# Stick-breaking attention: the scans' second operand moves to a PSUM column, and ScalarE copies the sums

## The chip, the cores and the metric

The kernel runs on one core of one Trainium2 chip. The metric is device time in microseconds (us), the median of the runs. The engines' names are those of the profile: PE (TensorE's matmuls), PEld (its weight loads), DVE (VectorE), ACT (ScalarE), POOL (GpSimd), SP (SyncE, which issues every DMA). PE writes only to PSUM, an accumulator memory of eight banks of 2 KB in each partition; DVE and ACT read it.

## The reference

One encoder layer for 2048 new frames (with 16 meta tokens ahead of them) and 64 frames of a running stream with 2048 cached ones: a combined projection, then two groups of heads, then an output projection and a gated ConvFFN. What matters here is group A, the stick-breaking attention: eight heads of 64, strictly causal, without a softmax.

```
z = (q @ k^T) * 64 ** -0.5                      # mask: key s < query t
log_1m = where(mask, log_sigmoid(-z), 0)
later  = cumsum(log_1m, reverse) - log_1m       # sum over the keys between s and t
a = where(mask, exp(log_sigmoid(z) + later), 0)
out = a @ v
```

So a weight is sigmoid(z) times the product of sigmoid(-z) over all keys that lie between key and query. Group B, the retention (four heads of 128), is a chunked recurrence and needs the same normalised input.

## The kernel before

The frames are stored newest first, so that the running product goes forward along a row. A matrix product at full precision is three matmuls of a high and a low part.

The stages follow each other: projections of q, k and v (to about 350 us), then a stage in which attention and retention are woven into one instruction stream (about 350 to 1320 us), then the rest of the retention with the output projection, then the ConvFFN. Every engine's queue is in program order, and the program order is written by hand: `attention()` and `retention()` are generators that yield the nanoseconds of PE work that they have just emitted, and `interleave` takes a step of retention (650 to 1300 ns nominal) whenever attention has got ahead of a fixed share, 0.82.

Attention is a list of 237 units: `Meta`, 20 `Samp` units (the running stream) and 216 `Prompt` units, one for a pair of heads p, a block I of 256 queries, a head e of the pair and a chunk of 512, 256 or 272 keys. By shape these are 48 units of 512 keys, 48 of 256 and 56 of 272 that continue a row, and 24 of 512, 32 of 256 and 8 of 272 that begin it (diagonal chunks, in which the second tile of queries skips 128 keys). A prompt unit goes through these steps:

- `z` (L1080 and after): for each of two tiles of 128 queries the matmuls of q and k into a PSUM tile `z` (L1094, L1095, L1097), then two sigmoids on ACT (`sigmoids`, L888), which write `sn` (of -z) and `sp` (of z) to SBUF. There is a yield behind each tile. Then comes `products`: two running products on DVE (`tensor_tensor_scan`, L898), one for each tile, and two multiplications `sp * pr` on POOL (L904).
- `t`: PE transposes the weights (L1123, L1126) into PSUM tiles `tt`; ACT copies each to `ahi` (L1116) and DVE makes the rest `alo` (L1117).
- `av`: 4 to 8 matmuls (L1157) add weights times values into `o`, a PSUM tile of 128x256 from the one-buffer pool `p_o`. Behind the last chunk of a row DVE copies `o` to `os` in SBUF (L1162), and the next row's first matmul has to wait for this copy.

The steps of different units are interleaved at fixed distances:

```
z = units[s].z() if 0 <= s < N else iter(())
yield next(z, 0)
for lag, what in ((3, "t"), (0, "z"), (4, "av"), (4, "fin"), (-2, "pre")):
```

So in program order the scans of unit s stand directly ahead of the `av` matmuls of unit s-4, and between `z` of the second tile and these scans stands at most what `interleave` puts at one yield. The scan computes state = data0 * state and bypasses its second operand, `data1`; before the change `data1` is `sn`, the same SBUF row as `data0`. The framework derives the semaphore waits from the tiles that instructions read and write.

Of the kernel before, what the change touches and what calls it, by code (L numbers as in the profile page):

```python
# [8 lines left out]
F32 = mybir.dt.float32  # L9
F32R = mybir.dt.float32r  # L10
BF16 = mybir.dt.bfloat16
AF = mybir.ActivationFunctionType
# [35 lines left out]
def hybrid_layer(ctx: ExitStack, tc: tile.TileContext, a):  # L48
# [5 lines left out]
    V, S, G, PE = nc.vector, nc.scalar, nc.gpsimd, nc.tensor  # L54
# [12 lines left out]
    def pool(stack, name, bufs, side="left", space=None):  # L67
        kw = {"space": space} if space is not None else {}
        return stack.enter_context(tc.tile_pool(name=name, bufs=bufs, reuse_waits="tile", side=side, **kw))
# [67 lines left out]
    while t > 0:  # L137
        n = min(GB, t)
# [533 lines left out]
    with ExitStack() as st:  # L672
# [10 lines left out]
        p_z = pool(st, "p2z", 2, space=PSUM)  # L683
        p_t = pool(st, "p2t", 2, space=PSUM)
        p_o = pool(st, "p2op", 1, space=PSUM)
        cos_t, sin_t, s_ret, tri_t = (p2[n] for n in ("cos", "sin", "s", "tri"))
        snr = [cp.tile([128, 2, 520], F32, name=f"sn{n}") for n in range(2)]
        qzs = [cp.tile([128, 2, 256], F32R, name=f"qz{n}") for n in range(3)]
# [123 lines left out]
        def attention():  # L812
# [4 lines left out]
            def piece_of(c):  # L817
                return min(c // 512, NPC - 1)
# [19 lines left out]
            def load_v(p, j):  # L838
                c0, c1 = edges[j], edges[j + 1]
                t0 = c0 // 128  # L840
                n = (c1 - c0) // 128
                vt = kvp.tile([128, -(-(c1 - c0) // 128), 256], F32R, name="vt", tag=f"v{j}")
                dma(out=vt[:, :n], in_=d_v[p, :, t0:t0 + n])
                if (c1 - c0) % 128:

                    G.memset(f32(vt[:, n]), 0.0)
                    dma(out=vt[:META, n], in_=d_v[p, :META, t0 + n])
                vpt[p, j] = vt

            def free_pieces(I):  # L850
                nxt = 256 * (I + 1)
                return [j for j in range(NPC) if edges[j + 1] == nxt or (nxt == SEQ and edges[j + 1] == KT)]
# [17 lines left out]
            class Breaks:  # L870
# [19 lines left out]
                def products(self, carry, nj=1):  # L890
                    n, sn, sp = self.n, self.sn, self.sp
                    pr = ppp.tile([128, 2, 520], F32, name="pr", tag="pr")
                    for j in range(nj):
                        s = self.skip * j
                        if s:
                            V.memset(pr[:, j, s:s + 1], 1.0)
                            s += 1
                        V.tensor_tensor_scan(  # L898
                            out=pr[:, j, s:n + 1], data0=sn[:, j, s:n + 1], data1=sn[:, j, s:n + 1],
                            initial=1.0 if carry is None else carry[:, j, 0:1], op0=ALU.mult, op1=ALU.bypass,  # L900
                        )
                    for j in range(nj):
                        c = slice(self.skip * j, n)
                        G.tensor_tensor(out=sp[:, j, c], in0=sp[:, j, c], in1=pr[:, j, c], op=ALU.mult)  # L904
                    return sp, pr[:, :, n:n + 1]
# [8 lines left out]
            class Meta:  # L914
# [21 lines left out]
                    yield 110  # L936

                def av(self):
                    self.o = p_o.tile([128, 256], F32, name="o", tag="o")
                    for p in range(NP):  # L940
                        PE.matmul(
                            self.o[32 * p:32 * p + 32, 0:128], lhsT=self.at[:, 32 * p:32 * p + 32],
                            rhs=v_last[0:META, 128 * p:128 * p + 128], start=True, stop=True,
                            tile_position=(0, 32 * p),
                        )
                    self.os = op.tile([128, 256], F32, name="os", tag="os", bufs=3)
                    V.tensor_copy(self.os[:, :128], self.o[:, :128])
                    yield 400
# [22 lines left out]
            def load_cv(g, j):  # L971
                cv = kvp.tile([128, 2, 4, 128], F32, name="cv", tag=f"v{j}")
                for e in range(2):
                    dma(out=cv[:, e], in_=a["cv"][2 * g + e, :, 4 * j:4 * j + 4])
                cvs[g, j] = cv

            class Samp:
# [45 lines left out]
                def av(self):  # L1023
                    p, c, st = self.p, self.c, self.st
                    if c == 0:
                        st["o", p] = p_o.tile([128, 256], F32, name="o", tag="o")
                        o = st["o", p]
                        PE.matmul(
                            o[:, :128], lhsT=self.at[:DEC, 0], rhs=v_samp[:, 128 * p:128 * p + 128],
                            start=True, stop=False,  # L1030
                        )
                    else:
                        o = st["o", p]
                        for b in range(4):
                            PE.matmul(
                                o[:, :128], lhsT=self.at[:, b], rhs=cvs[p // 2, c - 1][:, p % 2, b],
                                start=False, stop=c == NC and b == 3,
                            )
                        if p == 1:
                            load_cv(1, c - 1)  # L1040
                        elif p == 3 and c <= NPC:
                            load_v(0, c - 1)
                    if c == NC:
                        self.os = op.tile([128, 256], F32, name="os", tag="os", bufs=3)
                        V.tensor_copy(self.os[:, :128], o[:, :128])
                    yield 900
# [11 lines left out]
            class Prompt:  # L1058
# [80 lines left out]
                def av(self):  # L1139
                    p, e, st = self.p, self.e, self.st  # L1140
                    if self.c == 0:
                        st["o", e] = p_o.tile([128, 256], F32, name="o", tag="o")
                    o = st["o", e]
                    j0 = piece_of(self.start)
                    vt = vpt[p, j0]
                    b0 = (self.start - edges[j0]) // 128
                    seq = list(range(self.nb)) + ([self.nb] if self.rem else [])
                    if self.c == 0:
                        seq = seq[1:] + [0]
                    for x, b in enumerate(seq):  # L1150
                        w = 128 if self.c == 0 and b == 0 else 256
                        first = self.c == 0 and x == 0
                        end = self.c == self.nch - 1 and x == len(seq) - 1
                        vs = vt[:, b0 + b, 128 * e:128 * e + 128]
                        for z, src in enumerate((self.hi, self.lo)):
                            rhs = src[:, b].rearrange("p j c -> p (j c)")[:, :w]
                            PE.matmul(o[:, :w], lhsT=vs, rhs=rhs, start=first and z == 0, stop=end and z == 1)  # L1157
                        if x % 2 == 1:
                            yield 440
                    if self.c == self.nch - 1:  # L1160
                        self.os = op.tile([128, 256], F32, name="os", tag="os", bufs=3)
                        V.tensor_copy(self.os, o)  # L1162
                        if e == 1 and p + 1 < NP:
                            for j in free_pieces(self.I):
                                load_v(p + 1, j)
                    yield 220 * (len(seq) % 2)
# [21 lines left out]
            st = {}  # L1188
# [3 lines left out]
            for p in range(NP):  # L1192

                for I in [0] + list(range(NQ - 1, 0, -1)) if p == NP - 1 else range(NQ):
                    st = {}
# [600 lines left out]
```

## Time and profile before

| what | before |
|---|---|
| median of 3 runs (lowest, highest) | 3060.58 us (3058.88, 3062.67) |
| profiled execution, its span | 3063.43 us, 3061.7 us |
| PE busy | 2952.8 us, 96% |
| PEld busy | 2626.5 us, 86% |
| DVE busy | 2043.5 us, 67% |
| POOL busy | 1602.7 us, 52% |
| ACT busy | 1506.9 us, 49% |
| granted TensorE clock, mean | 0.991 |

Busy is the time in which an engine executed something. Matmuls are pipelined, so a matmul's record is longer than the distance to the next one; a busy PE is not PE at its peak. The granted clock is a share of 2.4 GHz. A timeline row gives the start in us from the span's start, the duration of what it merges, the engine, the line, the operation, what it wrote and read, and in brackets the idle time of the engine before it and what ended it.

### The profile page before, as it was taken

How to read it: one execution, taken by the hardware profiler on the slowest of the kernel's cores; microseconds unless marked ns; L12 is line 12 of the kernel's file. 1: busy time of each engine (PE TensorE's matmuls, PEld its weight loads, DVE VectorE, ACT ScalarE, POOL GpSimd, SP SyncE). 2: the span in 40 equal slices, each digit the busy share in tenths (PEclk: the TensorE clock that was granted, in tenths of full speed). 3: DMA queues.
4: the chain of work that ended last, by engine and by line, in shares of the span. 5: the costliest groups of instructions: out<-in, count | busy, mean ns of one | idle time of the engine just before them, and what ended most of it. 6: DMA issues, size and time to landing. Idle time of an engine off the chain costs nothing. (4 is left out here: it accounts for less than half of the span.)

```text
span 3061.7 us, 48809 instructions
## 1 busy us (share of the span) xinstructions
PE 2952.8 (96%) x16834; PEld 2626.5 (86%) x16834; DVE 2043.5 (67%) x3027; ACT 1506.9 (49%) x3331; POOL 1602.7 (52%) x1817
## 2 busy tenths in 40 slices
PE   7999999899999999999999999999999999999998
PEld 6888688788878878878789998789999889999887
DVE  3331368888888888854346666768888667888622
ACT  5332456666666666643334444454444444444433
POOL 1220377778778777753324445434446343455543
PEclk9999999999999999999999999999999999999999
DMA  6765753433343443247645556645555655455644
GB/s 224 279 221 178 263 176 104 134 119 105 122 136 103 126 129 107 75 173 252 212 155 178 185 176 229 199 158 152 154 157 170 220 187 164 148 146 155 212 156 149
DMA packets 278355, 512.07 MB, mean 167 GB/s; under 512 B 36612, under 2 KB 118404, under 8 KB 266204
## 3 DMA queue, kind: packets, MB, share of 16 engines
q1 hardware_dynamic: 278108, 508.95, 51.5%
q8 instruction: 134, 2.20, 0.3%
q14 instruction: 113, 0.93, 0.1%
HBM read 371.63 MB, written 137.09 MB: 166 GB/s over the span
## 5 line engine op out<-in xcount | busy, mean ns | idle before, releaser
L102 POOL TENSOR_TENSOR wl<-raw,wh 128x512 fp32r<-128x512 f32 x264 | 397.9, 1509 | 480.6 <-ACT wh L101 458.9
L904 POOL TENSOR_TENSOR sp<-sp,pr 128x272 f32<-128x272 f32 (+7 forms) x453 | 472.2, 1063 | 215.9 <-DVE pr L898 66.7
L101 ACT ACTIVATE wh<-raw 128x512 fp32r<-128x512 f32 x528 | 322.0, 623 | 222.9 <-DMA raw<-d_ws 132.1
L1473 PE MATMUL mm<-xs,wh 128*128 128x384 f32 x1232 | 411.5, 334 | 0.0
L1474 PE MATMUL mm<-xs,wl 128*128 128x384 f32 x1232 | 411.5, 334 | 0.0
L1472 PE MATMUL mm<-xs,wh 128*128 128x384 f32 x1232 | 411.5, 334 | 0.0
L898 DVE TENSOR_TENSOR_SCAN pr<-sn,pr 128x513 f32<-128x513 f32 (+2 forms) x320 | 338.1, 1095 | 29.4 <-ACT sn L888 22.0
L1402 DVE SCALAR_TENSOR_TENSOR c<-u,cw,c 128x768 f32<-128x768 f32 (+1 forms) x264 | 340.5, 1290 | 4.6 <-POOL u L1396 3.4
L1596 PE MATMUL mm<-wh,fl 128*128 128x512 f32 (+1 forms) x748 | 296.5, 396 | 8.6 <-DVE fl L102 8.4
L1594 PE MATMUL mm<-wh,fh 128*128 128x512 f32 (+1 forms) x748 | 294.3, 393 | 5.4 <-ACT fh L101 5.4
L1595 PE MATMUL mm<-wl,fh 128*128 128x512 f32 (+1 forms) x748 | 293.8, 393 | 0.0
L1117 DVE TENSOR_TENSOR alo<-tt,ahi 128x256 fp32r<-128x256 f32 (+3 forms) x496 | 218.4, 476 | 99.7 <-ACT ahi L1116 99.1
L102 DVE TENSOR_TENSOR fl<-fr,fh 128x768 fp32r<-128x768 f32 (+1 forms) x132 | 131.0, 993 | 215.2 <-ACT fh L101 204.0
L1408 POOL TENSOR_TENSOR c<-u,c 128x768 f32<-128x768 f32 (+1 forms) x66 | 118.1, 1789 | 264.8 <-ACT u L1407 264.8
L797 PE MATMUL dm<-wh,xt 128*128 128x512 f32 (+1 forms) x544 | 246.1, 452 | 5.2 <-ACT vtok L458 2.8
L101 ACT ACTIVATE fh<-fr 128x768 fp32r<-128x768 f32 (+1 forms) x132 | 105.2, 797 | 288.4 <-PE mm L1595 267.0
L102 DVE TENSOR_TENSOR wl<-raw,wh 128x512 fp32r<-128x512 f32 x264 | 199.0, 754 | 50.9 <-ACT wh L101 48.0
L1472 PEld LDWEIGHTS mm<-xs,wh 128*128 128x128 f32 x1232 | 231.3, 188 | 0.1
L1473 PEld LDWEIGHTS mm<-xs,wh 128*128 128x128 f32 x1232 | 231.3, 188 | 0.1
L1474 PEld LDWEIGHTS mm<-xs,wl 128*128 128x128 f32 x1232 | 231.3, 188 | 0.0
L1116 ACT ACTIVATE ahi<-tt 128x256 fp32r<-128x256 f32 (+3 forms) x496 | 193.5, 441 | 72.5 <-DVE alo L1117 51.4
L888 ACT ACTIVATE sn<-z 128x512 f32<-128x512 f32 (+2 forms) x360 | 169.3, 470 | 116.9 <-issue 51.3
(259 smaller groups left out, 7801.8 us busy)
## 6 DMA issues: line engine op xcount, KB each, us to landing
xt<-d_xt SPq DMA_DIRECT2D x68, 1024.0 KB
raw<-in_wup SPq DMA_DIRECT2D x220, 256.0 KB
raw<-d_ws SPq DMA_DIRECT2D x176, 256.0 KB
raw<-in_wdn SPq DMA_DIRECT2D x132, 256.0 KB
fr<-d_f SPq DMA_DIRECT2D x88, 384.0 KB
d_ws<-raw SPq DMA_DIRECT2D x88, 256.0 KB
d_xt<-xt SPq DMA_DIRECT2D x17, 1024.0 KB
d_f<-c SPq DMA_DIRECT2D x44, 384.0 KB
```

Of the source, the lines that this page charges most:

```text
L101: S.activation(out=hi, in_=raw, func=AF.Copy)
L102: lo_engine.tensor_tensor(out=lo, in0=raw, in1=hi.bitcast(F32), op=ALU.subtract)
L797: PE.matmul(ps[:r], lhsT=xt[:, 0, k, :r], rhs=wh, start=k == 0, stop=False)
L898: V.tensor_tensor_scan(out=pr[:, j, s:n + 1], data0=sn[:, j, s:n + 1], data1=sn[:, j, s:n + 1], initial=1.0 if carry is None else carry[:, ...
L904: G.tensor_tensor(out=sp[:, j, c], in0=sp[:, j, c], in1=pr[:, j, c], op=ALU.mult)
L1402: V.scalar_tensor_tensor(out=cvs[e][:, :W], in0=u[:, 2 - y:W + 2 - y], scalar=cw[:, ch, y:y + 1], in1=cvs[e][:, :W], op0=ALU.mult, op1=ALU ...
L1472: PE.matmul(ps, lhsT=wh[:, w], rhs=x[:, 0], start=k == 0, stop=False)
L1473: PE.matmul(ps, lhsT=wh[:, w], rhs=x[:, 1], start=False, stop=False)
L1474: PE.matmul(ps, lhsT=wl[:, w], rhs=x[:, 0], start=False, stop=k == 3)
L1594: PE.matmul(pss[x][:r], lhsT=fh[:, c], rhs=wh, start=k == 0, stop=False)
L1595: PE.matmul(pss[x][:r], lhsT=fh[:, c], rhs=wl, start=False, stop=False)
L1596: PE.matmul(pss[x][:r], lhsT=fl[:, c], rhs=wh, start=False, stop=k == NF - 1)
```

## The change

One PSUM tile of a whole bank, `o_bank`, takes the place of the tiles `o` that were allocated for each row. Columns 0 to 255 hold the sums as before; column 511 is set to 1.0 once and is read by every scan as `data1`, broadcast along the row. The copy of a prompt row's finished sums goes from DVE to ACT.

```
+        o_bank = p_o.tile([128, 512], F32, name="o")
+        V.memset(o_bank[:, 511:512], 1.0)
...
                         V.tensor_tensor_scan(
-                            out=pr[:, j, s:n + 1], data0=sn[:, j, s:n + 1], data1=sn[:, j, s:n + 1],
+                            out=pr[:, j, s:n + 1], data0=sn[:, j, s:n + 1],
+                            data1=o_bank[:, 511:512].to_broadcast([128, n + 1 - s]),
...
-                    self.o = p_o.tile([128, 256], F32, name="o", tag="o")
+                    self.o = o_bank[:, :256]
...
-                        st["o", p] = p_o.tile([128, 256], F32, name="o", tag="o")
+                        st["o", p] = o_bank[:, :256]
...
-                        st["o", e] = p_o.tile([128, 256], F32, name="o", tag="o")
+                        st["o", e] = o_bank[:, :256]
...
-                        V.tensor_copy(self.os, o)
+                        S.activation(out=self.os, in_=o, func=AF.Copy)
```

## Rows read from the trace of the kernel before

**Rows 1.** Windows view: busy time of each engine in the woven stage; columns named first.
```profile
core 0: us, PE busy (x) PEld busy (x) DVE busy (x) ACT busy (x) POOL busy (x), PEclk, DMA share, GB/s
440.00:1320.00 880.00, 825.24 (x5396) 717.76 (x5395) 740.47 (x1398) 579.69 (x1681) 681.22 (x829) 0.99 0.35 113
```

**Rows 2.** View of line L765, what DVE waited for before it (us, times).
```profile
  PE ro L763: 14.9, 12
```

**Rows 3.** View of the tile ahi, what its engines waited for before it (us, times).
```profile
  DVE alo L1117: 51.4, 64
```

**Rows 4.** Groups of DVE instructions, 440 to 1320 us: count | busy us, mean ns | idle before.
```profile
L898 DVE TENSOR_TENSOR_SCAN pr<-sn,pr 128x513 f32<-128x513 f32 x92 | 123.6, 1385 | 0.0
L898 DVE TENSOR_TENSOR_SCAN pr<-sn,pr 128x257 f32<-128x257 f32 x94 | 93.1, 1031 | 0.0
L898 DVE TENSOR_TENSOR_SCAN pr<-sn,pr 128x273 f32<-128x273 f32 x110 | 89.2, 852 | 0.0
...
L1162 DVE COPY os<-o 128x256 f32<-128x256 f32 x63 | 25.1, 398 | 0.0
...
L898 DVE TENSOR_TENSOR_SCAN pr<-sn 128x128 f32<-128x128 f32 x32 | 18.2, 570 | 0.0
```

**Rows 5.** Timeline of PE, 885 to 899 us: first sum matmuls of four successive units.
```profile
885.57 0.28 PE L1157 MATMUL o<-ahi,vt 128*128 128x256 f32 x1
...
889.92 0.28 PE L1157 MATMUL o<-ahi,vt 128*128 128x256 f32 x1
...
894.95 0.37 PE L1157 MATMUL o<-ahi,vt 128*128 128x256 f32 x1
...
898.96 0.28 PE L1157 MATMUL o<-ahi,vt 128*128 128x256 f32 x1
```

**Rows 6.** Timeline of DVE there: the pair of scans written ahead of each of them.
```profile
886.37 1.39 DVE L898 TENSOR_TENSOR_SCAN pr<-sn,pr 128x257 f32<-128x257 f32 x2
...
890.59 1.46 DVE L898 TENSOR_TENSOR_SCAN pr<-sn,pr 128x273 f32<-128x273 f32 x2
...
895.52 2.10 DVE L898 TENSOR_TENSOR_SCAN pr<-sn 128x513 f32<-128x513 f32 x2
...
899.64 2.46 DVE L898 TENSOR_TENSOR_SCAN pr<-sn,pr 128x513 f32<-128x513 f32 x2
```

**Rows 7.** Timeline of PE, 958 to 971 us: first sum matmuls of four successive units.
```profile
958.62 0.37 PE L1157 MATMUL o<-ahi,vt 128*128 128x256 f32 x1
...
963.35 0.28 PE L1157 MATMUL o<-ahi,vt 128*128 128x256 f32 x1
...
967.70 0.28 PE L1157 MATMUL o<-ahi,vt 128*128 128x256 f32 x1
...
970.90 0.28 PE L1157 MATMUL o<-ahi,vt 128*128 128x256 f32 x1
```

**Rows 8.** Timeline of DVE there: the pair of scans written ahead of each of them.
```profile
960.33 2.09 DVE L898 TENSOR_TENSOR_SCAN pr<-sn 128x513 f32<-128x513 f32 x2
...
963.31 3.17 DVE L898 TENSOR_TENSOR_SCAN pr<-sn,pr 128x513 f32<-128x513 f32 x2
...
968.97 2.16 DVE L898 TENSOR_TENSOR_SCAN pr<-sn,pr 128x257 f32<-128x257 f32 x2
...
972.10 2.11 DVE L898 TENSOR_TENSOR_SCAN pr<-sn,pr 128x273 f32<-128x273 f32 x2
```

**Rows 9.** Timeline of PE, 814 to 816 us: a wait and the matmuls behind it.
```profile
814.43 0.38 PE L1157 MATMUL o<-ahi,vt 128*128 128x256 f32 x1 [1.59 <-DVE os L1162]
...
815.19 0.63 PE L797 MATMUL dm<-wh,xt 128*128 128x512 f32 x1
815.62 0.63 PE L798 MATMUL dm<-wl,xt 128*128 128x512 f32 x1
```

**Rows 10.** Windows view of the stretch behind that wait; columns as in Rows 1.
```profile
814.80:818.10 3.30, 3.30 (x13) 2.90 (x12) 2.79 (x5) 0.81 (x3) 2.58 (x4) 0.50 0.35 94
```

**Rows 11.** Groups of ACT instructions, 440 to 1320 us; columns as in Rows 4.
```profile
L1116 ACT ACTIVATE ahi<-tt 128x256 fp32r<-128x256 f32 x310 | 109.5, 390 | 60.9 <-DVE alo L1117 51.0 <-PE tt L1123 4.8 <-PE tt L1126 4.4
```

## The prediction, made before the changed kernel ran

> **What bounds the kernel now.** I read the windows view first, cut at the stages, because only the woven stage of attention and retention contains what is changed. There, from 440 to 1320 us, PE is busy 825.24 of 880 us at a granted clock of 0.99, while DVE is busy 740.47, POOL 681.22 and ACT 579.69 [rows 1]. So the stage is PE's: only 880 - 825 = 55 us of it are PE's idle time, and DVE is the next engine, at 84%. Then I read the groups of DVE in that stage: none of the scans has idle time ahead of it, so they stand in a queue that is always filled [rows 4]. Then I read the timeline of PE beside that of DVE, to see how far DVE runs behind PE. This is what decides the case: at present nothing makes the sum matmuls of unit s-4 wait for the scans of unit s, which stand just ahead of them in program order, and PE is already through them when those scans run.
>
> **Does the change make them wait?** The scans now read column 511 of the bank whose columns 0 to 255 the sum matmuls write. No column is shared, so the question is whether waits are made by columns or by bank. Two places of the trace before tell. The retention's L765 reads columns 0 to 127 of a PSUM tile, which L756 and L762 write; L763, the next matmul, writes columns 128 to 255 of the same bank. DVE waited for L763, 12 times and 14.9 us in all [rows 2]: a read waits for a write of other columns. And where a 272-key unit has two copies out of one PSUM tile `tt`, the second L1116 on ACT waited for DVE's L1117 on the first one's columns, 64 times and 51.4 us [rows 3], though both only read the bank. There are 56 + 8 = 64 units of 272 keys. So every two engines on one bank are put in order, whatever they touch.
> The Trainium skill says the same of the chip (PSUM — Partial Sum Buffer, section PSUM bank collisions raise a hardware error): two engines in one bank and one quarter of the partitions must be ordered by semaphores even at disjoint columns, and two readers too. By that rule alone the first rival below has no chance, and what I forecast follows whatever the gain in the scans.
>
> **What the new wait costs.** In program order the scans of s come ahead of the sums of s-4, so the first of these matmuls waits until the second scan of s has ended. PE is in order: behind that matmul wait all later ones, the retention's fill and z of unit s+1. The other direction is free: a scan of s+1 must wait for the sums of s-4, but these run before z of s+1 on PE, which the scan needs anyway.
>
> The price for one unit is the end of its scan pair less the start of the sum matmuls that do not yet wait for it. Lowest that I saw, in four successive units with the scans next to undisturbed [rows 5, 6]:
> - 256 keys: 886.37 + 1.39 - 885.57 = 2.19 us
> - 272 keys: 890.59 + 1.46 - 889.92 = 2.13 us
> - 512 keys, diagonal: 895.52 + 2.10 - 894.95 = 2.67 us
> - 512 keys: 899.64 + 2.46 - 898.96 = 3.14 us
>
> For a short diagonal chunk, whose second scan has 128 columns, I take 2.19 less the difference of the two means, 1.031 - 0.570 = 0.46 [rows 4]: 1.73 us. With the counts of units: 48 x 2.19 + 56 x 2.13 + 24 x 2.67 + 48 x 3.14 + 40 x 1.73 = 105 + 119 + 64 + 151 + 69 = 508 us.
>
> In four successive units with DVE's usual backlog [rows 7, 8] the same differences are 3.80 (512, diagonal), 3.13 (512), 3.43 (256) and 3.31 (272). With 3.43 - 0.46 = 2.97 for the short diagonals: 91 + 150 + 165 + 185 + 119 = 710 us.
>
> Which of the two? Once PE pauses in each unit, DVE and ACT get that time to run their queues empty, so the backlog shrinks towards the first four. I take 508 and a quarter of the way to 710: 559 us. The 20 units of the running stream have one scan each, emitted further ahead of the sums; at one scan of 513, 1.385 us [rows 4], that is 28 us.
>
> **What it gives back.** A scan that reads one SBUF row in place of two: the 257-column scan has a mean of 1.031 us [rows 4], and the pair in 1.39 us is 0.70 each [rows 6]; for 273 it is 0.85 against 0.73. That is stretching by POOL's reads, and most of it is already gone in the lower prices above. Its largest worth on DVE is 94 x 0.33 + 110 x 0.12 + 92 x (1.385 - 1.23) = 31 + 13 + 14 = 58 us; as the scans are now on PE's path, this is the difference between 710 and some 650, and it is one reason for taking a value near the lower end. That a PSUM column costs a scan extra is not shown; the nearest rows, DVE's copy of 128x256 out of PSUM in 398 ns [rows 4] and two columns' scans above, let me bound it by 0.1 us either way: 216 x 2 x 0.1 = 43 us. I take 0.
> The copy of the sums, 63 x 0.398 = 25 us of DVE [rows 4], becomes as many ACT copies at about 0.390, the time of an ACT copy of that shape out of PSUM [rows 11]. ACT is free 300 of 880 us [rows 1]; the copy is behind the sums and ahead of sigmoids that wait for later matmuls, so I cost it at 0. Without that cover it would be 25 us, and the gain is at most as much. PE's wait for this copy (1.59 us in the example [rows 9]) goes, but what is late next is the scan pair, which ends later still. PE's 55 us of present idle time [rows 1] fall together with the new waits; I subtract 45. The one memset is nothing.
>
> **The clock.** After PE had waited 1.59 us at 814.43, matmuls of 512 columns came every 0.43 us [rows 9], and the granted clock of 814.8 to 818.1 is 0.50, the 1.2 GHz level [rows 10]. Such a stretch loses 3.3 x 0.5 = 1.65 us of PE's work. The stage's mean of 0.99 [rows 1] says it is rare now; with a pause of 1.7 to 3.1 us in every unit I expect it behind about half of 236 units, and some two thirds of it to fall where PE would have waited for the scans in any case: 118 x 1.65 x 0.55 = 107 us. The ends are 0 and 236 x 1.65 = 389 us.
>
> **Sum**, against the profiled execution of 3063.4 us: + 559 + 28 - 45 + 107 = + 649, so 3712; the median of the runs lies 2.9 us lower, so 3710 us.
>
> **Rivals.**
> 1. *Waits go by columns* (the other side). Then nothing waits, scans and POOL's multiplications get out of each other's way, and at most PE's idle 55 us go: half of them is 3063 - 28 = 3035 us. For it: PE writes and DVE reads no common column. Against it: both places where the bank was put in order [rows 2, 3]. The Trainium skill (SBUF — State Buffer, section Who interferes with whom) gives the reason why the scans would be quicker: a DVE instruction with two SBUF inputs contends with POOL's reads, one with a single SBUF input doesn't. The trace's 1.031 against 0.70 us agrees. Worth at most the 58 us of DVE above, on an engine that is not the bound. Chance 0.05.
> 2. *DVE keeps up.* With empty queues the first scan runs before PE ends z of the second tile, and only the second scan is left: half of each lower pair, 48 x 1.23 + 56 x 0.73 + 48 x 0.70 + 24 x 1.05 + 40 x 0.57 = 59 + 41 + 34 + 25 + 23 = 182 us. With 28, less 45, and 40 for the clock: 3270 us. For it: a first scan needs only the first tile's sigmoid. Against it: even in the lowest four the pair began 0.57 to 0.80 us after the sums [rows 5, 6], as `alo` of the transposes stands ahead of it on DVE. Chance 0.11.
> 3. *The clock stays low.* With PE at 1.2 GHz for the stage its 825 us become 1650, and about half of the waits (280 us) lie beside that: 3063 - 880 + 1650 + 280 = 4110 us. For it: a pause in each unit. Against it: behind each pause comes a burst of 4 us of PE's work (825 / 216 = 3.8). Chance 0.08.
>
> **Chances.** The forecast, a wait in nearly every unit at 3450 to 3950 us, has 0.76. The range that holds the time 8 times in 10 is 3440 to 3990: it leaves out rivals 1 and 2 and most of 3. The upper end is 3063 + 710 + 28 + 190 for the clock. About 0.2% (6 us) is what a measurement tells from no change. Faster by more: 0.04, all from rival 1; within it: 0.01; slower: 0.95.
>
> **What would show it.** In the profile after: PE's line L1157 has idle time ahead of it in the order of 500 us or more, ended by DVE `pr` L898, about 230 times, where it was ended by `os`; a sum matmul never starts before the scan pair written ahead of it has ended; PE's busy share falls only in the woven stage, which grows to some 1500 us, with stretches of granted clock at half. The scans of 257 columns fall to about 0.7 us; L1162 moves to ACT at about 0.39 us. The stages ahead of 350 us and behind the woven stage keep their length. I am wrong if L1157 has no such wait, or if the woven stage keeps its length with it.

## The result, and the profile after

| what | before | changed |
|---|---|---|
| median of 4 runs (lowest, highest) | 3061.62 us (3058.88, 3064.63) | 3750.37 us (3744.01, 3762.15) |
| ratio to before, 95% interval | 1 | 1.2254 (1.2221 to 1.2286) |
| span of the profiled execution | 3061.7 us | 3760.3 us |
| granted TensorE clock, mean | 0.991 | 0.931 |

The change makes the kernel 689 us slower; 3710 us was forecast, in a range of 3440 to 3990. The changed kernel's lines are numbered a few higher: the scan is L901 (L898 before), POOL's multiplication L908 (L904), the sum matmul L1161 (L1157), the copy of the sums L1166 (L1162), `alo` L1121, the z matmuls L1098 and L1099.

The windows view of the changed kernel, with the stage ahead of the woven one, the woven stage and the ConvFFN; columns as in [rows 1]:

```profile
core 0: us, PE busy (x) PEld busy (x) DVE busy (x) ACT busy (x) POOL busy (x), PEclk, DMA share, GB/s
0.00:350.00 350.00, 327.57 (x1581) 277.19 (x1581) 104.93 (x135) 121.44 (x230) 66.98 (x97) 0.97 0.68 236
...
440.00:2013.00 1573.00, 1069.97 (x5465) 903.01 (x5464) 671.65 (x1345) 626.84 (x1765) 553.45 (x838) 0.85 0.20 65
...
2190.00:3761.00 1571.00, 1545.50 (x8514) 1423.52 (x8512) 1070.03 (x1297) 695.00 (x1177) 726.13 (x737) 1.00 0.55 172
```

Nearly the whole loss is in the woven stage: 1573 us against 880 [rows 1], +693. It has two parts. PE's idle time went from 880 - 825 = 55 us to 1573 - 1070 = 503: +448. And PE's busy time went from 825 to 1070 us, +245, for nearly the same matmuls (5465 records against 5396): the granted clock fell from 0.99 to 0.85, and 1573 x 0.15 = 236 us.

The waits of PE in the changed kernel (us in total, times, longest) say who ended the idle time. Before, nearly all waits of the sum matmuls were for `os` (an example is in [rows 9]):

```profile
PE o L1161 <- DVE pr L901: 498.1, 212, 4.4
PE o L1039 <- DVE pr L901: 15.3, 13, 2.7
...
PE o L1032 <- DVE pr L901: 1.8, 4, 1.0
...
PE o L945 <- DVE pr L901: 1.3, 1, 1.3
```

Together 516 us, at 230 places. One of them, in the timelines of PE, DVE and POOL in the changed kernel:

```profile
1196.28 0.39 PE L1161 MATMUL o<-ahi,vt 128*128 128x256 f32 x1 [1.73 <-DVE pr L901]
1196.51 0.28 PE L1161 MATMUL o<-alo,vt 128*128 128x256 f32 x1
1196.62 0.28 PE L1161 MATMUL o<-ahi,vt 128*128 128x256 f32 x1
...
1197.81 0.57 PE L1098 MATMUL z<-kt,q 128*128 128x272 f32 x1
1198.19 0.43 PE L1099 MATMUL z<-kt,qz 128*128 128x272 f32 x1
1200.83 0.58 PE L1161 MATMUL o<-ahi,vt 128*128 128x256 f32 x1 [2.22 <-DVE pr L901]
...
1202.28 0.63 PE L801 MATMUL dm<-wl,xt 128*96 128x512 f32 x1
1202.71 0.63 PE L802 MATMUL dm<-wh,xt 128*96 128x512 f32 x1
```

```profile
1199.33 1.45 DVE L901 TENSOR_TENSOR_SCAN pr<-sn,pr,o 128x273 f32<-128x273 f32 x2
```

```profile
1200.25 1.48 POOL L908 TENSOR_TENSOR sp<-sp,pr 128x272 f32<-128x272 f32 x2 [2.47 <-DVE pr L901]
```

The reader is to see three things. The z matmul of the second tile ends at 1198.62, and the next instruction of PE is the sum matmul, 2.2 us later. It starts 0.05 us after the pair of scans has ended (1199.33 + 1.45 = 1200.78); the scans have `o` among their operands. And the matmuls of 512 columns behind it come every 0.43 us, as in [rows 9]: at half clock.

The clock was at half already ahead of this pause, as the windows view shows (columns as above):

```profile
1197.00:1200.70 3.70, 1.61 (x8) 1.29 (x6) 1.91 (x4) 2.06 (x6) 1.23 (x4) 0.50 0.89 366
1200.90:1204.00 3.10, 3.10 (x13) 2.64 (x14) 0.00 (x0) 0.20 (x1) 1.78 (x5) 0.55 0.01 3
1204.30:1207.70 3.40, 2.58 (x19) 2.05 (x17) 1.47 (x5) 2.61 (x8) 0.00 (x0) 1.00 0.00 0
```

Behind the pause before (1.73 us) the first sums still came 0.11 us apart, at full clock; then the clock fell, and it stayed low through the next pause. So a stretch of low clock does not begin and end with one pause. The trace's record of the clock has 117 such stretches in this stage, 481 us in all.

The scans themselves got quicker. Groups of DVE, POOL and ACT in the changed kernel, in the form of [rows 4], over the whole span:

```profile
L901 DVE TENSOR_TENSOR_SCAN pr<-sn,pr,o 128x513 f32<-128x513 f32 x112 | 138.2, 1269 | 38.0 <-ACT sn L891 32.4 <-POOL t L730 2.0 <-POOL t L735 2.0
...
L901 DVE TENSOR_TENSOR_SCAN pr<-sn,pr,o 128x273 f32<-128x273 f32 x112 | 81.5, 767 | 1.6 <-ACT sn L891 1.5
...
L901 DVE TENSOR_TENSOR_SCAN pr<-sn,pr,o 128x257 f32<-128x257 f32 x96 | 66.8, 735 | 1.0 <-ACT sn L891 1.0
...
L908 POOL TENSOR_TENSOR sp<-sp,pr 128x512 f32<-128x512 f32 x136 | 171.8, 1278 | 346.5 <-DVE pr L901 190.1 <-DVE pr L899 109.5 <-ACT gate L719 26.8
...
L1166 ACT ACTIVATE os<-o 128x256 f32<-128x256 f32 x64 | 24.6, 384 | 159.1 <-PE o L1161 159.0
```

A scan of 257 columns takes 0.735 us (1.031 [rows 4]), one of 513 takes 1.269 (1.385). That shortens the new waits, but it removes none: DVE now is busy 672 of 1573 us and waits, with ACT and POOL, for a PE that waits for them. How much of it is the PSUM column's doing is seen in the experiments.

### The profile page after: what moved, and what is told of

It is laid out like the page before. It is cut to its first block, busy times and chain, and to the rows that moved or that the text cites. A ratio compares the mean times of both kernels' runs of the same rounds, so it can differ in the third digit from the quotient of the medians.

```text
span 3760.3 us, 48829 instructions
## 1 busy us (share of the span) xinstructions
PE 3189.5 (85%) x16834; PEld 2801.7 (75%) x16834; DVE 1959.2 (52%) x2964; ACT 1545.7 (41%) x3395; POOL 1457.7 (39%) x1817
## 5 line engine op out<-in xcount | busy, mean ns | idle before, releaser
L908 POOL TENSOR_TENSOR sp<-sp,pr 128x272 f32<-128x272 f32 (+7 forms) x453 | 396.2, 894 | 870.8 <-DVE pr L901 530.5
L1161 PE MATMUL o<-ahi,vt 128*128 128x256 f32 (+1 forms) x640 | 216.4, 357 | 498.1 <-DVE pr L901 498.1
L1161 PEld LDWEIGHTS o<-ahi,vt 128*128 128x128 f32 x640 | 143.5, 224 | 558.6 <-DVE pr L901 540.3
L1121 DVE TENSOR_TENSOR alo<-tt,ahi 128x256 fp32r<-128x256 f32 (+3 forms) x496 | 221.1, 481 | 632.6 <-ACT ahi L1120 631.8
L901 DVE TENSOR_TENSOR_SCAN pr<-sn,pr,o 128x513 f32<-128x513 f32 (+2 forms) x320 | 286.5, 933 | 40.6 <-ACT sn L891 34.9
L800 PE MATMUL dm<-wh,xt 128*128 128x512 f32 (+1 forms) x544 | 281.1, 517 | 5.1 <-DMA xt<-d_xt 2.9
L801 PE MATMUL dm<-wl,xt 128*128 128x512 f32 (+1 forms) x544 | 246.5, 453 | 0.0
L802 PE MATMUL dm<-wh,xt 128*128 128x512 f32 (+1 forms) x544 | 246.2, 453 | 0.0
```

Of the source, the lines that this page charges most:

```text
L901: V.tensor_tensor_scan(out=pr[:, j, s:n + 1], data0=sn[:, j, s:n + 1], data1=o_bank[:, 511:512].to_broadcast([128, n + 1 - s]), initial=1. ...
```

## The experiments

The theory: the bank alone puts each unit's sums behind its scans; this wait, and the low clock that follows such a pause, are the whole loss. The rivals: the new operand, or ScalarE's copy, costs the time; or any lockstep of DVE and PE does; or the low clock is hidden beside the waits.

**The constant column in SBUF** (the changed kernel, one thing put back):

```
-        V.memset(o_bank[:, 511:512], 1.0)
+        one_col = cp.tile([128, 1], F32, name="one_col")
+        V.memset(one_col, 1.0)
...
-                            data1=o_bank[:, 511:512].to_broadcast([128, n + 1 - s]),
+                            data1=one_col.to_broadcast([128, n + 1 - s]),
```

> The changed kernel with one thing put back: the constant column lies in SBUF, not in the bank of the sums; the scans still read a broadcast column, and ScalarE still copies the sums. Theory (the wait of the sum matmuls for the scans is made by the shared bank alone, and it and the low clock behind it are all of the 690 us): no wait of L1157's counterpart for a scan, and 3040 to 3075 us. Rival (the new form of operand or ScalarE's copy costs the time): 3400 us or more. Open in both: whether a column in SBUF still counts as a second SBUF input; if so the 257-column scans stay near 1.03 us, if not they fall to 0.7 and POOL's multiplications get shorter too.

Measured: 3047.33 us, 0.9949 of before (0.9937 to 0.9962). PE waits for no scan. So the column's place in the bank of the sums is the cause, and neither ScalarE's copy, nor the broadcast operand, nor the one tile that all rows of sums now share.

No run tells the bank from the PSUM tile: the kernel gives each of its PSUM tiles in this stage a bank of its own (2 + 1 + 2 + 2 + 1 of eight), so that both say the same. But a tile as such is not put in order here: in the timeline above POOL begins at 1200.25 to multiply the first half of `pr`, in SBUF, while DVE's second scan still writes the other half until 1200.78.

The scans of this run, in the same view:

```profile
L902 DVE TENSOR_TENSOR_SCAN pr<-sn,pr,one_col 128x513 f32<-128x513 f32 x112 | 153.9, 1409 | 28.8 <-ACT sn L892 20.0 <-POOL t L731 3.9 <-POOL sp L909 2.6
...
L902 DVE TENSOR_TENSOR_SCAN pr<-sn,pr,one_col 128x257 f32<-128x257 f32 x96 | 100.0, 1082 | 0.0
```

1.082 us for 257 columns: a single column in SBUF stretches the scan as a whole row does.

**ScalarE's copy alone** (the kernel before with `V.tensor_copy(self.os, o)` replaced by the activation).

> The kernel before with one part of the change alone: ScalarE copies a row's sums. Theory (hidden, as PE's waits for this copy are 18 us and ACT has free time): 3050 to 3070 us, within 0.3% of before. Rival (ACT is in order, and a copy that waits for the sums holds up the sigmoids behind it): 64 copies at 0.4 to 2 us, 3085 to 3190 us.

Measured: 3043.15 us, 0.9943 (0.9930 to 0.9955): faster by 17 us, more than either theory had. In the woven stage of before (the first two lines, 340 to 1320 us), PE waited 18.3 us for DVE's `os` at the sums and 7.0 at the transposes; with the copy on ACT (the third line) the sums wait 2.6 us for it:

```profile
PE o L1157 <- DVE os L1162: 18.3, 20, 2.0
...
PE tt L1130 <- DVE os L1162: 7.0, 3, 3.4
...
PE o L1157 <- ACT os L1162: 2.6, 2, 1.5
```

On DVE the copy had stood behind a pair of scans.

**The scans behind the sums** (the changed kernel, prompt units). `products` leaves `z` and becomes a step `pr` of its own:

```
-                for lag, what in ((3, "t"), (0, "z"), (4, "av"), (4, "fin"), (-2, "pre")):
+                for lag, what in ((3, "t"), (0, "z"), (4, "av"), (0, "pr"), (4, "fin"), (-2, "pre")):
```

> The changed kernel with one thing moved: the prompt units' scans are emitted behind the sum matmuls of the same step, not ahead of them, so that sums wait for scans of a whole step earlier, and scans wait for the sums just ahead. Theory (it is the place of the wait, 3.2 us too early for DVE, that costs): the next sums come 4.1 us later on average in the kernel before, so most waits go: 0 to 60 us left, clock at 0.98 or more, 3030 to 3110 us. Rival (any lockstep of DVE and PE in each unit costs about as much, as scans now wait for sums): 3400 us or more.

Measured: 3072.05 us, 1.0035 (1.0022 to 1.0048). The same sharing, with the wait one step later in program order, leaves the kernel 12 us above before, not 690; what the sharing still costs is seen below, against a control. Waits of PE between 340 and 1320 us:

```profile
PE o L1167 <- DVE pr L901: 42.1, 48, 2.3
PE o L1039 <- DVE pr L901: 7.4, 9, 1.4
```

So it isn't lockstep as such that costs 690 us, but that the wait came one step too early for DVE.

**The control: the same move in the kernel before.**

> The kernel before with the same move alone, without the PSUM column and with DVE's copy: the control of the run on late scans. Nothing shares a bank here. Theory: the move by itself delays scans by the sums' 0.5 to 1 us, which the distance of three steps to the transposes covers: 3050 to 3080 us. If the PSUM column is worth something once its wait is out of the way, the run with it is below this one, by at most 30 us.

Measured: 3039.72 us, 0.9929 (0.9917 to 0.9941), faster than expected. With the scans behind the sums, DVE's copy of the sums no longer queues behind them, and PE's waits for `os` fall from 18.3 and 7.0 us to 2.0 and 0.6. The run with late scans is 32 us above this control, but it also has ScalarE's copy. Against the same order with that copy (3033.98 us, the run with the two parts together, below), the PSUM column costs 38 us even with the wait well placed.

The scans of 257 columns in these two runs, first without the PSUM column and then with it:

```profile
L898 DVE TENSOR_TENSOR_SCAN pr<-sn,pr 128x257 f32<-128x257 f32 x96 | 96.4, 1044 | 0.0
...
L901 DVE TENSOR_TENSOR_SCAN pr<-sn,pr,o 128x257 f32<-128x257 f32 x96 | 66.6, 736 | 15.6 <-ACT os L1172 8.9 <-PE o L1167 2.1 <-POOL sp L908 1.9
```

Here, where few pauses are left, such a scan takes 0.31 us less with the column.

**Only the first scan of a pair reads the bank.**

```
-                            data1=o_bank[:, 511:512].to_broadcast([128, n + 1 - s]),
+                            data1=sn[:, j, s:n + 1] if j else o_bank[:, 511:512].to_broadcast([128, n + 1 - s]),
```

> The changed kernel with the second scan of each pair reading sn again: the sums wait for the first scan only. Theory (the wait is the distance from the sums to the end of the last scan on the bank): each unit's wait falls by about one scan, 0.4 to 1.25 us, 216 units by some 0.85: 180 us fewer waits of the 516, and with a shorter pause fewer stretches at the lower clock: 3450 to 3580 us. Rival (a fixed price for each wait, whatever its length): within 60 us of 3750.

Measured: 3495.91 us, 1.1426 (1.1409 to 1.1443). PE's waits:

```profile
PE o L1161 <- DVE pr L901: 268.1, 152, 3.3
PE o L1161 <- DVE pr L899: 91.8, 58, 2.7
PE o L1039 <- DVE pr L901: 11.1, 12, 1.6
```

(L899 is the 0.06 us memset behind the first scan of a diagonal chunk.) The sum matmuls' waits fall by 498 - 360 = 138 us, somewhat less than the 180 expected. The windows view gives the clock, 0.92 over 1308 us where it was 0.85 over 1569, so 105 us lost instead of 235:

```profile
440.00:1748.00 1308.00, 941.78 (x5440) 793.62 (x5440) 681.50 (x1344) 617.12 (x1760) 635.90 (x837) 0.92 0.24 78
```

138 + 130 = 268, of 254 measured. That the two add up is near to bookkeeping, as they are PE's idle and its slow time. What refutes a fixed price for each wait is that nearly as many waits (210 against 212 at L1161) cost over a third less: the price is the length of the wait plus the clock that it brings.

The run shows one thing more. Its scans of 257 columns and POOL's multiplication, and below them the same multiplication in the kernel before:

```profile
L901 DVE TENSOR_TENSOR_SCAN pr<-sn,pr 128x257 f32<-128x257 f32 x48 | 35.8, 747 | 0.6 <-ACT sn L891 0.6
L901 DVE TENSOR_TENSOR_SCAN pr<-sn,pr,o 128x257 f32<-128x257 f32 x48 | 35.6, 741 | 0.0
...
L908 POOL TENSOR_TENSOR sp<-sp,pr 128x512 f32<-128x512 f32 x136 | 216.8, 1608 | 278.0 <-DVE pr L901 147.5 <-DVE pr L899 83.6 <-ACT gate L719 30.5
...
L904 POOL TENSOR_TENSOR sp<-sp,pr 128x512 f32<-128x512 f32 x136 | 214.7, 1594 | 121.4 <-DVE pr L898 35.0 <-DVE pr L896 20.0 <-ACT gate L716 14.8
```

The second scans, which read two SBUF rows again, still take 0.747 us. So where PE pauses in each unit, the scans are quick with either operand, and their fall from 1.031 to 0.735 us in the changed kernel does not by itself show what the column does. In this run it is POOL that follows the operand: 1.608 us, as before (1.594), where the changed kernel has 1.278.

**Work in the wait** (the changed kernel, with matmuls that nothing uses ahead of the scans and the sums of each prompt unit).

```
+                    for _ in range(16):
+                        PE.matmul(zs[0][:, :256], lhsT=identb, rhs=maskb.rearrange("p n c -> p (n c)"), start=True, stop=True)
```

> The changed kernel with work added: 16 extra bf16 matmuls of 256 columns (about 1.7 us of PE at full clock) in each prompt unit, just ahead of the sums, into the first z tile, whose sigmoids are done; their results are not used. They run where PE would have waited. Theory (a part of the loss, some 200 us, is not the wait but matmuls at half clock behind it, and this part is not hidden under the waits): the clock in the woven stage goes from 0.85 to 0.97 or more, and the kernel gets faster although PE does more: 3520 to 3660 us. Rival (the time at the lower clock lies beside the wait for DVE and costs nothing): 3750 us or more.

Measured: 3603.84 us, 1.1773 (1.1755 to 1.1791): with 3456 matmuls more it is 147 us faster than the changed kernel. Its windows view, its wait at the sums, and the added matmuls:

```profile
440.00:1855.00 1415.00, 1252.81 (x8887) 1056.11 (x8885) 668.55 (x1344) 615.55 (x1763) 553.47 (x839) 0.99 0.22 72
```

```profile
PE o L1163 <- DVE pr L901: 155.7, 162, 2.6
```

```profile
L1105 PE MATMUL z<-maskb,identb 128*128 128x256 bf16 x3456 | 414.0, 273 | 3.7 <-ACT sp L891 3.3
```

The clock is 0.99. The added work is about 3456 x 256 columns / 2.4 GHz = 370 us (an estimate; its records are busy for 414, each being longer than the distance to the next), of which 498 - 156 = 342 us lay in waits that were there. So the clock gave back about 147 + 28 = 175 us by the first figure, 147 + 72 = 219 by the second, of the 221 that its share lost (235 - 14): most of it had lain on the path, not beside the waits.

**A bank of its own.** All eight banks are in use in this stage, so one was taken from the retention's projections, first without anything else:

```
-        p_d = pool(st2r, "p2d", 2, space=PSUM, side="right")
+        p_d = pool(st2r, "p2d", 1, space=PSUM, side="right")
```

> The kernel before with one PSUM bank taken from the retention's projections (one buffer, not two): the base for the next run. Every step of the retention must then wait for the readers of the one before: 3070 to 3250 us.

and then with the constant column in the bank set free:

> As the run with one retention buffer, and the scans read the constant column from the bank that this sets free, which nothing else uses; DVE copies the sums as before. Theory (reading a PSUM column is harmless and takes the scans off the port that POOL reads through): no wait for scans, the 257-column scans at 0.70 us, and 0 to 55 us below the run with one retention buffer. Rival (a PSUM operand in itself slows scans or sums): 100 us or more above that run.

Measured: 3222.15 us, 1.0523 (1.0498 to 1.0547), and 3187.05 us, 1.0405 (1.0388 to 1.0423). Reading a PSUM column that shares no bank takes 35 us off, without any wait for a scan; the 257-column scans are at 0.734 us (0.938 in the base, the first line):

```profile
L898 DVE TENSOR_TENSOR_SCAN pr<-sn,pr 128x257 f32<-128x257 f32 x96 | 86.4, 938 | 2.8 <-ACT sn L888 2.8
...
L901 DVE TENSOR_TENSOR_SCAN pr<-sn,pr,cb 128x257 f32<-128x257 f32 x96 | 66.8, 734 | 4.8 <-ACT sn L891 4.8
```

So the idea behind the change gains something on this base, where PE waits 72 us for DVE's `gate` of the retention. What it lacks is a free bank, and making one this way costs 161 us; what it would be worth in the kernel before, with a bank to spare, no run shows.

**The two parts that helped, together** (ScalarE's copy and the prompt scans behind the sums, no PSUM column).

> Two parts that were each faster alone, together, and no PSUM column: prompt scans emitted behind the sums, and ScalarE's copy of the sums. If both gains (17 us for the copy, 21 us for the move) come from different waits they add: 3015 to 3030 us. If both only shorten the same backlog of DVE, the sum is not reached: 3030 to 3042 us.

Measured: 3033.98 us, 0.9914 (0.9900 to 0.9927): 28 us below before and the fastest version. The gains of 17 and 21 us add only in part, since both remove the same waits for `os`.

**Late scans, with only the prompt units on the bank.**

> The run with late scans, with the 20 running-stream units' scans (which were not moved) reading sn again, so that only prompt units share the bank. Theory: the stage of the running stream gets back the 16 us that it had lost against the control, and the rest stays, 43 us of waits against what the freed port gives: 3050 to 3062 us. So the PSUM column would still not beat the same order without it (3040 us). If the freed port were worth more than the waits: under 3040 us.

Measured: 3060.39 us, 0.9995 (0.9986 to 1.0003): no change against before, and 26 us above the run just before, which has the same order and ScalarE's copy but no column. The running stream's units, whose scans had stayed ahead of their sums, had cost the run with late scans 12 us.

## Why the prediction was right, and where its sizes were off

- *That the bank is put in order.* Right; read from a wait for a matmul that wrote other columns [rows 2] and from two readers of one bank [rows 3], and shown by moving the constant out of the bank: 3750 to 3047 us.
- *The price of a wait.* The lower prices of [rows 5, 6] were the right ones: they gave 508 us for the prompt units, and the profile after has 498.1. They hold shape by shape, worked out from the idle time at L1161 and the scans ahead of it: 2.04 us for 256 keys (2.19 forecast), 2.29 for 272 (2.13), 2.66 for 512 diagonal (2.67), 3.13 for 512 (3.14), and 1.7 for the short diagonals (1.73). Going a quarter of the way towards [rows 7, 8], to 559, was the mistake. Behind each pause DVE, ACT and POOL had emptied their queues, so a backlog like that of before never built up; DVE fell from 84% busy to 672 of 1573 us, 43%. The running stream's units cost 17 us in all instead of 28, and only 4.9 of it behind 440 us. All 55 us of PE's earlier idle time went, not 45. So 542 us were forecast for PE's added idle time in this stage; it is 498.1 + 4.9 - 55 = 448.
- *The clock.* 107 us forecast, 245 measured in PE's busy time. The number of slow stretches was right, 117 for 118. Their length was not: 481 us in all cost 240, where 118 x 1.65 = 195 were reckoned. But the step that failed most is the factor 0.55, by which slow matmuls were to lie beside the wait for the scans. (The prediction's words don't fit it either: if two thirds lay beside the wait, a third would be left, 65 us.) Most of them don't: z of the second tile stands ahead of the sigmoids and scans on that same PE, so a slow z delays the scans as much as the sums. The run with work in the wait shows the size: 175 to 219 of 221 us came back, 0.8 to 1 of it; that z is the way it goes is argued from the program's order and not tested by itself.
- These two sizes were wrong in opposite directions (94 us too much, 138 too little). That the sum came within 40 us is luck; with either of the two alone put right it would have been 3616 or 3848, still in the range.
- *What it gives back.* The scans did fall, 1.031 to 0.735 us, though behind such pauses they are nearly as quick with two SBUF rows (0.747 us). The column's worth was seen where no wait for it stands in the way, 35 us in the bank of its own; 58 us of DVE's time had been named as the most.
- *The copy.* Costed at 0 with a gain of at most 25 us; alone it gains 17. What hid the gain in the changed kernel is that the scan pair ends later than the copy had.
- *Rivals.* Columns instead of banks: refuted. DVE keeping up (3270 us): refuted, 2.2 us of wait at a 272-key unit and 0.7 us between the end of z and the scans' start, in the timeline above. The clock low for the whole stage (4110 us): refuted, 0.85.

## What to carry to other kernels

Before an operand is put into the unused half of a PSUM bank, list who writes and reads that bank and in which program order: every pair of engines there gets a wait, and an instruction early in the order with a slow predecessor stops an in-order PE for all that follows. Price such a wait from the timeline of before as the distance by which the two now overlap, at an undisturbed place, and add the clock that PE loses behind the pause. If the sharing is kept, place the reader behind the writer in the program, so that the next writer comes a step later; here even that cost 38 us against the same order without sharing.

## What the runs showed of the hardware that was not expected

A broadcast of one column in SBUF stretches a scan beside POOL's work as much as a whole row (1.082 us for 257 columns; 1.083 with the row in the run with ScalarE's copy alone), while a column in PSUM does not (0.736 with late scans, where the row takes 1.044). Where a scan with two SBUF operands started ahead of POOL's multiplication, behind a pause, it was POOL that took longer (1.608 us against 1.278) and the scan did not (0.747). PE's clock here depended on its idle time to the point that some 370 us of useless matmuls made the kernel 147 us faster.
